# Order of the high and low products in the gate and up projections of a hybrid decoder layer

## The chip, the cores and the metric

The kernel runs on one core of a Trainium2 chip. The metric is the device time of one execution in microseconds (us). Three runs of the kernel before took 1007.79, 1008.01 and 1008.3 us; their median, 1008.01 us, is the time before.

The engines are named as the profile names them: PE is TensorE's matrix products, PEld its weight loads, DVE is VectorE, ACT is ScalarE, POOL is GpSimd, SP is the engine whose queue issues most loads. A "product" is one matmul instruction: 128 x 128 weights, with 256 or 512 columns of activations streamed past them.

## The reference

One decoder layer on 256 tokens of 2048 features, in float32:

```
h = RMSNorm(x);  z = h @ w_in
y = concat(pool mixer, latent attention of 8 heads, attention of 4 heads to 256 memory tokens) @ w_o
x = x + y
h2 = RMSNorm(x)
g = h2 @ w_gate ;  gc = conv_b + sum over j of conv_w[j] * (g shifted by 2 - j tokens)
x = x + (silu(gc) * (h2 @ w_up)) @ w_down
```

`w_gate` and `w_up` are 2048 x 5632, `w_down` is 5632 x 2048. With 44 features tiles of 128 columns, gate and up are 44 x 2 x 16 blocks of 128 x 128 weights.

## The kernel before

**High and low.** Every operand of the large products is split into a high part, rounded to the type fp32r, and a low part, the rest. A product is made of three: high weight by high activation, high weight by low activation, and low weight by high activation. The activations `h2` lie in SBUF as 256 high columns followed by 256 low columns, so that a *high product* (`psm<-h,wh`) streams 512 columns past a block of high weights, and a *low product* (`psm<-h,wl`) streams 256 columns past a block of low weights and adds to the second half of the same PSUM bank. `halves` (L767 on) adds the two halves later.

**From memory to weights.** `load_w` (L82) brings 128 x 2048 floats, 1 MB, into one of three buffers `wr` by SP's queue: a whole features tile of gate or of up. It is split in two pieces of 1024 columns, eight blocks each. For each piece ScalarE writes `wh` by a copy that rounds (L98), and VectorE subtracts it from the raw weights into `wl` (L99). There are three buffers `wh` and three buffers `wl`; a piece occupies one of each until its last product has read it.

**Where the low piece starts.** A buffer `wl` is 64 floats longer than a piece. `gemm_t` (L103) puts the first low piece of a features tile 48 floats (192 bytes) into its buffer and the second one 16 floats (64 bytes). All other weights start at the beginning of their buffers.

**Order.** `gemm_t` runs the first piece high, then low, and the second low, then high. Up follows gate with the same order:

| | piece 0 | piece 1 |
|---|---|---|
| gate | 8 high, 8 low | 8 low, 8 high |
| up | 8 high, 8 low | 8 low, 8 high |

So the loop over f (L817) is a sequence of runs of 16 high and 16 low products. Tile f=0 is done in two parts: the first pieces of gate and up, then the last transposes of the activations, then the second pieces. The input projections (ten features tiles of `w_z`, with the activations `xg`) use `gemm_t` too, and between their two pieces steps of the memory attention are put.

**After a features tile.** `glu` (L774) takes the two PSUM banks: ScalarE copies and VectorE adds the halves (L770, L771), scales, does the three-tap convolution (L778, L780), silu (L781) and the product with up. In 13 of the 22 pairs of features tiles the result is split into `aT` (L144, L145). In the nine pairs of `SEVEN` the second tile of the pair also makes sums and differences of 128 x 128 blocks (`s<-s`, L799) and splits 896 columns at once into `aS` (L802, L803), for a down projection with seven block products where eight would be plain.

**What sets the order of instructions.** Each engine works through its own queue in order. A planner fills the queues ahead of time: it plays the program through with estimated durations, and each engine takes the earliest instruction in the program's order that is ready, including a free buffer for its output. An instruction marked by `keep` stays behind everything written before it on its engine. The gate and up products, splits and `glu` are not marked. PSUM has four banks `psm`, so that gate and up of two features tiles can be under way.

**Other names.** `rxb` (the input's scale for every token, used by the pool mixer) and `krr` (the rotated rope keys) are small tiles of the pool `mix`. `ssacc` is the buffer in which the squares of the memory tokens are summed.

Of the kernel before, what the change touches and what calls it, by code (L numbers as in the profile page):

```python
# [11 lines left out]
F32 = mybir.dt.float32  # L12
F32R = mybir.dt.float32r
BF16 = mybir.dt.bfloat16
AF = mybir.ActivationFunctionType
ALU = mybir.AluOpType
AX = mybir.AxisListType

P = 128
T = 256  # L20
NT = 2
D = 2048
KD = D // P
H = 8
NOPE = 128
ROPE = 64
# [10 lines left out]
STG = 2048  # L37
HS = 1024
# [22 lines left out]
def layer(ctx, tc, xT_d, xn_d, memT_d, vec_d, tab_d, w_z_d, w_mqkr_d, w_q_d, w_kv_d, w_mem_d, w_pool_d, w_o_d,  # L61
          w_g_d, w_u_d, w_dn_d, out_d):
    nc = tc.nc

    const = ctx.enter_context(tc.tile_pool(name="const", bufs=1))
    stage = ctx.enter_context(tc.tile_pool(name="stage", bufs=1))
# [5 lines left out]
    def nm(s):  # L72
        uid[0] += 1
        return f"{s}_{uid[0]}"

    def ps_main():
        return psm.tile([P, 512], F32, tag="m", name=nm("psm"))

    def ps_aux():
        return psa.tile([P, 512], F32, tag="a", name=nm("psa"))  # L80

    def load_w(src, n, cut=STG):  # L82
        raw = stage.tile([P, STG], F32, tag="wr", name=nm("wr"), bufs=3)
        for c in range(0, n, cut):
            nc.sync.dma_start(raw[:, c:min(n, c + cut)], src[:, c:min(n, c + cut)])
        return raw[:]

    def keep(ins, on=True):

        return tc.keep_in_program_order(ins) if on else ins  # L90

    def split_w(raw, o, n, cut=HS, kept=False, shift=0):

        hi = stage.tile([P, HS], F32R, tag="wh", name=nm("wh"), bufs=3)
        lo = stage.tile([P, HS + 64], F32R, tag="wl", name=nm("wl"), bufs=3)[:, shift:shift + HS]
        for c in range(0, n, cut):
            e = min(n, c + cut)
            keep(nc.scalar.copy(hi[:, c:e], raw[:, o + c:o + e]), kept)  # L98
            keep(nc.vector.tensor_tensor(lo[:, c:e], raw[:, o + c:o + e], hi[:, c:e].bitcast(F32), op=ALU.subtract),  # L99
                 kept)  # L100
        return hi, lo

    def gemm_t(ps, raw, o, act, ks, first=True, last=True, kept=False, between=None):  # L103


        ks = list(ks)
        nk = HS // P
        cs = range(0, len(ks), nk)
        for c in cs:
            kc = ks[c:c + nk]  # L110

            hi, lo = split_w(raw, o + c * P, len(kc) * P, shift=16 if c // nk % 2 else 48)

            for low in ((False, True) if c // nk % 2 == 0 else (True, False)):
                for i, k in enumerate(kc):
                    w = (lo if low else hi)[:, i * P:(i + 1) * P]
                    keep(nc.tensor.matmul(ps[:, T if low else 0:2 * T], w, act(k)[:, 0:T] if low else act(k),  # L117
                                          start=first and c + i == 0 and not low,
                                          stop=last and c == cs[-1] and i == len(kc) - 1 and low == (c // nk % 2 == 0),
                                          skip_group_check=True), kept)  # L120
            if between is not None and c == 0:
                between()

    def gemm_n(pss, hi, lo, act, k0, first, last, kept=False, by_span=False):

        nk, n = hi.shape[1], hi.shape[2]
        nj = len(pss[0])
        w = n // nj
        order = [(tt, j) for tt in range(NT) for j in range(nj)]
        if by_span:  # L130
            order.sort(key=lambda x: x[1])
        for i in range(nk):
            for tt, j in order:
                xh = act[:, k0 + i, tt * P:(tt + 1) * P]
                xl = act[:, k0 + i, T + tt * P:T + (tt + 1) * P]
                ps, o = pss[tt][j], slice(j * w, (j + 1) * w)
                keep(nc.tensor.matmul(ps, xh, hi[:, i, o], start=first and i == 0, stop=False), kept)  # L137
                keep(nc.tensor.matmul(ps, xl, hi[:, i, o], start=False, stop=False), kept)  # L138
                keep(nc.tensor.matmul(ps, xh, lo[:, i, o], start=False, stop=last and i == nk - 1), kept)  # L139
# [26 lines left out]
    def rsqrt_(dst, src, scale):  # L166

        nc.scalar.activation(dst, src, AF.Sqrt, bias=eps[:], scale=scale)
        nc.vector.reciprocal(dst, dst)
# [3 lines left out]
    mp = mix.enter_context(tc.tile_pool(name="mix", bufs=1))  # L173
# [7 lines left out]
    def sm(n):  # L181
        o = so[0]
        so[0] += n
        return small[:, o:o + n]

    def tok():
        return mp.tile([P, 512], F32, tag="tok", name=nm("tok"), bufs=3)
# [30 lines left out]
    def head_sq(dst, src):  # L218

        sq = mp.tile([P, 512], F32, tag="hsq", name=nm("hsq"), bufs=2)  # L220
        s3 = sq[:, :src.shape[1] * src.shape[2]].rearrange("p (h d) -> p h d", h=src.shape[1])
        nc.scalar.activation(s3, src, AF.Square)
        nc.vector.tensor_reduce(dst, s3, axis=AX.X, op=ALU.add)
# [31 lines left out]
    ps = ps_aux()  # L255
# [24 lines left out]
    pss = [[ps_main()[:] for _ in range(2)] for _ in range(NT)]  # L280
    for c in range(KD // 2):
        raw = raw0 if c == 0 else load_w(w_mem_d[c], STG, HS if c == 1 else STG)
# [4 lines left out]
        for i in range(2):  # L287
            k = 2 * c + i
            mem_parts(k, k + 1)
            hi, lo = split_w(raw, i * HS, HS, 512 if c == 0 else HS, True)  # L290
# [8 lines left out]
    ps = ps_aux()  # L299
# [41 lines left out]
    def x_load():  # L341
        i = len(x_pieces)
        sq = s4()[:].rearrange("p a t -> p (a t)")
        nc.gpsimd.dma_start(sq, xn_d[i // 2][:, (i % 2) * HS:(i % 2 + 1) * HS])
        x_pieces.append(sq)
# [5 lines left out]
    def x_rstd():  # L351
        keep(nc.vector.tensor_reduce(rx, ssq_x.rearrange("p (t h) -> p t h", h=2), axis=AX.X, op=ALU.add))
        rsqrt_(rx, rx, 1.0 / D)
        nc.vector.tensor_tensor(rx2, rx, rx, op=ALU.mult)
# [6 lines left out]
    pss = [[ps_aux()[:, :NH] for _ in range(2)] for _ in range(NT)]  # L361
    for c in range(KD // 2):
        raw = load_w(w_mqkr_d[c], 2 * 576)
        for i in range(2):
            hi, lo = split_w(raw, i * 576, 576)
# [9 lines left out]
            x_square(i)  # L375
        if c < 4:
            x_load()
    rxb = mp.tile([P, T], F32, name="rxb")

    def mq_done():  # L380

        x_rstd()
        for tt in range(NT):
            t = tok()
            nc.scalar.copy(t[:, 0:NH], pss[tt][0][:, :NH])
            nc.scalar.copy(t[:, NH:512], pss[tt][1][:, :512 - NH])
            nc.scalar.copy(kr[:, tt, :], pss[tt][1][:, 512 - NH:NH])
            head_sq(fmq3[:, tt], t[:].rearrange("p (h d) -> p h d", d=XD))
            nc.vector.tensor_scalar(fmq3[:, tt], fmq3[:, tt], rx2[:, tt:tt + 1], None, op0=ALU.mult)
            to_features(mqT, t, tt, XH, gqk[:, 1:2])  # L390
        rsqrt_(fmq, fmq, 1.0 / XD)
        for tt in range(NT):
            nc.vector.tensor_scalar(fmq3[:, tt], fmq3[:, tt], rx[:, tt:tt + 1], 1.0 / math.sqrt(XD),
                                    op0=ALU.mult, op1=ALU.mult)


        dx = tok()
        for tt in range(NT):
            nc.vector.tensor_scalar(dx[:, tt * P:(tt + 1) * P], identf[:], rx[:, tt:tt + 1], None, op0=ALU.mult)
        ps = ps_aux()  # L400
        nc.tensor.matmul(ps[:, 0:T], ones[:], dx[:, 0:T], start=True, stop=True)
        nc.scalar.copy(rxb[:], ps[:, 0:T])


    class Head:
# [75 lines left out]
    for m in range(6):  # L481
        raw = load_w(w_z_d[m], STG)
        if m in (1, 3):
            keep(nc.sync.dma_start(x1n[:, m // 2, :], xn_d[m // 2]))
        ps = ps_main()
# [3 lines left out]
        a = zs[:, m // 4, :]  # L489
        if m % 4 == 0:  # L490
            nc.scalar.activation(a, z[:], AF.Square)
        else:
            t = mp.tile([P, T], F32, tag="hadd", name=nm("zsq"), bufs=3)
# [21 lines left out]
    zp = mp.tile([P, 4, T], F32, name="zp")  # L515
    def pool_in(g):
        raw = load_w(w_z_d[6 + g], STG)
        ps = ps_main()
        gemm_t(ps, raw, 0, lambda k: xg[:, k, :], range(KD), kept=g == 0, between=lambda: mem_steps(6 + g))
        half_add(zp[:, g, :], ps)  # L520
        nc.vector.tensor_tensor(zp[:, g, :], zp[:, g, :], rxb[:], op=ALU.mult)


    def pool_mix():
# [60 lines left out]


    sskr, fk, fkn, fkr = sm(NT), sm(NT * H), sm(NT * H), sm(NT * H)
    krr = mp.tile([P, NT, 1, ROPE], F32, name="krr")
    for tt in range(NT):
        head_sq(sskr[:, tt:tt + 1], kr[:, tt:tt + 1, :])  # L590
        rotate(krr[:, tt], kr[:, tt:tt + 1, :], 1, tt, 1)
# [119 lines left out]
    for n in range(4):  # L711
        pss = [[ps_main()[:]] for _ in range(NT)]
# [7 lines left out]
    h2 = big.tile([P, KD, 2 * T], F32R, tag="act", name="h2")  # L720
# [17 lines left out]
    for n in range(4):  # L738
        pss = [[ps_main()[:]] for _ in range(NT)]
# [66 lines left out]
    raws = [load_w(w[0], STG) for w in (w_g_d, w_u_d)]  # L806
    pss = [ps_main() for _ in range(2)]
# [7 lines left out]
        gemm_t(ps, raw, HS, lambda k: h2[:, k, :], range(8, KD), first=False)  # L815
    glu(0, *pss)
    for f in range(1, KF):  # L817
        pss = []
        for w in (w_g_d, w_u_d):
            raw = load_w(w[f], STG)  # L820
            pss.append(ps_main())
            gemm_t(pss[-1], raw, 0, lambda k: h2[:, k, :], range(KD))
        glu(f, *pss)


# [85 lines left out]
    for c in range(2):  # L911
# [3 lines left out]
        for j in range(PAIRS):  # L915
            kept = c > 0 or j > SEVEN[0]
# [99 lines left out]
```

## Time and profile before

| | |
|---|---|
| median of three runs | 1008.01 us |
| the profiled execution | 1008.52 us |
| its span, first to last instruction | 1006.7 us |
| TensorE busy (products) | 1001.2 us, 99% |
| TensorE weight loads | 863.2 us, 86% |
| VectorE busy | 751.4 us, 75% |
| ScalarE busy | 577.8 us, 57% |
| memory traffic | 198 GB/s over the span |
| high products of gate and up (L117, `h,wh`) | 1408, mean 391 ns |
| low products of gate and up (L117, `h,wl`) | 1408, mean 278 ns |

How to read it: a product's duration counts from its start to the end of its way through the array, and the next product starts long before that. So the mean durations of 391 and 278 ns are not what a product costs; that is the time from one start to the next. A line such as `L99 DVE TENSOR_TENSOR wl<-wr,wh 128x1024 ... x172 | 210.5, 1224` is a group of instructions: line of the program, engine, operation, output and inputs, shape, count, busy microseconds, mean nanoseconds. A row of the windows is a stretch in microseconds from the span's start, its length, the busy time and count of an engine, the granted TensorE clock, the share of the DMA engines and GB/s. A row of the timeline is a start, a length, an engine, a line and an operation, with the number of instructions merged into it, and in brackets the engine's idle time before it and what ended that.

### The profile page before, as it was taken

How to read it: one execution, taken by the hardware profiler on the slowest of the kernel's cores; microseconds unless marked ns; L12 is line 12 of the kernel's file. 1: busy time of each engine (PE TensorE's matmuls, PEld its weight loads, DVE VectorE, ACT ScalarE, POOL GpSimd, SP SyncE). 2: the span in 40 equal slices, each digit the busy share in tenths (PEclk: the TensorE clock that was granted, in tenths of full speed). 3: DMA queues.
4: the chain of work that ended last, by engine and by line, in shares of the span. 5: the costliest groups of instructions: out<-in, count | busy, mean ns of one | idle time of the engine just before them, and what ended most of it. 6: DMA issues, size and time to landing. Idle time of an engine off the chain costs nothing.

```text
span 1006.7 us, 14129 instructions
## 1 busy us (share of the span) xinstructions
PE 1001.2 (99%) x5354; PEld 863.2 (86%) x5354; DVE 751.4 (75%) x1134; ACT 577.8 (57%) x853; POOL 18.5 (2%) x39
## 2 busy tenths in 40 slices
PE   9999999999999999999999999999999999999998
PEld 8898888888888888888888888888888888888886
DVE  6878689855677676776767677676767788888886
ACT  6778666544576555555555555555555565545553
POOL 1010000000000000000000000000000000010000
PEclk9999999999999999999999999999999999999999
DMA  9777344334665555554555555555555765576551
GB/s 361 260 243 297 129 165 178 128 146 145 210 208 210 179 197 193 184 208 172 205 184 195 194 184 209 174 203 185 191 200 201 263 214 191 205 275 212 206 209 42
DMA packets 31764, 200.17 MB, mean 199 GB/s; under 512 B 3664, under 2 KB 4176, under 8 KB 9808
## 3 DMA queue, kind: packets, MB, share of 16 engines
q1 hardware_dynamic: 28512, 189.04, 52.9%
q0 software_dynamic: 2752, 9.44, 2.6%
q8 instruction: 42, 0.69, 0.3%
q10 hardware_dynamic: 432, 0.79, 0.3%
q14 instruction: 26, 0.21, 0.1%
HBM read 195.06 MB, written 4.19 MB: 198 GB/s over the span
## 4 chain that ended last, share of the span: by engine, by line
PE 99%; DVE 0%; ACT 0%; issue 0%
PE psm L117 53%; PE psm L137 5%; PE psm L138 5%; PE psm L139 5%; PE psa L846 4%; PE psm L844 4%; PE psm L845 4%; PE psa L844 4%; PE psa L845 4%; PE psm L846 4%; PE psa L665 1%; PE psa L137 1%; PE psa L139 1%; PE psa L138 1%; PE psa L229 1%; PE psa L257 1%
## 5 line engine op out<-in xcount | busy, mean ns | idle before, releaser
L99 DVE TENSOR_TENSOR wl<-wr,wh 128x1024 fp32r<-128x1024 f32 (+2 forms) x338 | 392.3, 1165 | 63.7 <-ACT wh L98 58.7
L98 ACT CAST wh<-wr 128x1024 fp32r<-128x1024 f32 (+2 forms) x338 | 339.4, 1006 | 136.2 <-PE psm L138 47.3
L117 PE MATMUL psm<-h,wh 128*128 128x512 f32 x1408 | 336.8, 391 | 0.0
L117 PEld LDWEIGHTS psm<-h,wh 128*128 128x128 f32 x1408 | 257.7, 188 | 50.0
L117 PEld LDWEIGHTS psm<-h,wl 128*128 128x128 f32 x1408 | 176.1, 188 | 6.9
L117 PE MATMUL psm<-h,wl 128*128 128x256 f32 x1408 | 177.5, 278 | 0.0
L99 DVE TENSOR_TENSOR wl<-dn,wh 128x1024 fp32r<-128x1024 f32 x58 | 67.8, 1220 | 26.3 <-ACT wh L98 26.3
L98 ACT CAST wh<-dn 128x1024 fp32r<-128x1024 f32 x58 | 59.3, 1052 | 38.3 <-PE psm L845 21.7
L770 ACT COPY g<-psm 128x256 f32<-128x256 f32 x44 | 16.4, 372 | 88.7 <-PE psm L117 88.7
L771 DVE TENSOR_TENSOR g<-g,psm 128x256 f32<-128x256 f32 x44 | 18.5, 420 | 58.7 <-ACT g L770 58.7
L771 DVE TENSOR_TENSOR u<-u,psm 128x256 f32<-128x256 f32 x44 | 18.5, 421 | 52.8 <-ACT u L770 52.8
L781 ACT ACTIVATE gc<-gc 128x256 f32<-128x256 f32 x44 | 18.4, 419 | 63.9 <-DVE gc L780 63.8
L780 DVE SCALAR_TENSOR_TENSOR gc<-g,vec,gc 128x255 f32<-128x255 f32 x88 | 42.1, 478 | 0.3
L844 PE MATMUL psa<-wh,aT 128*128 128x512 f32 x104 | 40.5, 389 | 0.0
L845 PE MATMUL psa<-wh,aT 128*128 128x512 f32 x104 | 40.5, 389 | 0.0
L845 PE MATMUL psm<-wh,aT 128*128 128x512 f32 x104 | 40.5, 389 | 0.0
L846 PE MATMUL psa<-wl,aT 128*128 128x512 f32 x104 | 40.5, 389 | 0.0
L844 PE MATMUL psm<-wh,aT 128*128 128x512 f32 x104 | 40.5, 389 | 0.0
L846 PE MATMUL psm<-wl,aT 128*128 128x512 f32 x104 | 40.5, 389 | 0.0
L117 PE MATMUL psm<-xg,wh 128*128 128x512 f32 x160 | 39.9, 393 | 0.0
L137 PE MATMUL psm<-wh,cat 128*128 128x512 f32 x96 | 38.2, 398 | 0.0
L139 PE MATMUL psm<-wl,cat 128*128 128x512 f32 x96 | 37.4, 390 | 0.0
(227 smaller groups left out, 1393.9 us busy)
## 6 DMA issues: line engine op xcount, KB each, us to landing
wr<-in_w_g SPq DMA_DIRECT2D x44, 1024.0 KB, 4.8
wr<-in_w_u SPq DMA_DIRECT2D x44, 1024.0 KB, 4.8
wr<-in_w_dn SPq DMA_DIRECT2D x33, 1024.0 KB, 4.8
wr<-in_w_o SPq DMA_DIRECT2D x16, 1024.0 KB, 4.9
dn<-in_w_dn SPq DMA_DIRECT2D x11, 1024.0 KB, 4.9
wr<-in_w_z SPq DMA_DIRECT2D x10, 1024.0 KB, 5.5
wr<-in_w_mem SPq DMA_DIRECT2D x6, 1024.0 KB, 7.8
wr<-in_w_mqkr SPq DMA_DIRECT2D x8, 576.0 KB, 4.0
```

The costliest lines, as they stand in the source:

```text
L98: keep(nc.scalar.copy(hi[:, c:e], raw[:, o + c:o + e]), kept)
L99: keep(nc.vector.tensor_tensor(lo[:, c:e], raw[:, o + c:o + e], hi[:, c:e].bitcast(F32), op=ALU.subtract), kept)
L117: keep(nc.tensor.matmul(ps[:, T if low else 0:2 * T], w, act(k)[:, 0:T] if low else act(k), start=first and c + i == 0 and not low, stop=l ...
L137: keep(nc.tensor.matmul(ps, xh, hi[:, i, o], start=first and i == 0, stop=False), kept)
L138: keep(nc.tensor.matmul(ps, xl, hi[:, i, o], start=False, stop=False), kept)
L139: keep(nc.tensor.matmul(ps, xh, lo[:, i, o], start=False, stop=last and i == nk - 1), kept)
L771: nc.vector.tensor_tensor(t[:], t[:], ps[:, T:2 * T], op=ALU.add)
L780: nc.vector.scalar_tensor_tensor(gc[:, d:T], g[:, 0:T - d], v(w, f), gc[:, d:T], op0=ALU.mult, op1=ALU.add)
L781: nc.scalar.activation(gc[:], gc[:], AF.Silu)
L844: nc.tensor.matmul(ps, a[0], b[0], start=first, stop=False)
L845: nc.tensor.matmul(ps, a[1], b[0], start=False, stop=False)
L846: nc.tensor.matmul(ps, a[0], b[1], start=False, stop=last)
```

## The change

For the tiles f = 1 to 43 a new function `gemm_pair` does gate and up together. Each is split whole, and then gate runs 16 high and 16 low products and up 16 low and 16 high:

| | |
|---|---|
| gate | 16 high, 16 low |
| up | 16 low, 16 high |

A new function `split_t` replaces `split_w` in `gemm_t` and serves `gemm_pair`. It writes a low piece in two halves of four blocks, by one subtraction whose output has a gap, and each half has its own offset in the buffer, given modulo 64 floats. The first low piece of gate (and the first of each `gemm_t`) has its first half at 192 bytes and its second half at 64 bytes more than a multiple of 256; all other low pieces have both halves at 64. The buffers `wl` grow by 64 floats to 1152. To make room, `rxb` and `krr` move into one tile `late` that takes the buffer of `ssacc`.

```diff
-    def split_w(raw, o, n, cut=HS, kept=False, shift=0):
+    def split_w(raw, o, n, cut=HS, kept=False):
...
-        lo = stage.tile([P, HS + 64], F32R, tag="wl", name=nm("wl"), bufs=3)[:, shift:shift + HS]
+        lo = stage.tile([P, HS + 128], F32R, tag="wl", name=nm("wl"), bufs=3)[:, 0:HS]
...
+    def split_t(raw, o, n, low, kept):
+        hi = stage.tile([P, HS], F32R, tag="wh", name=nm("wh"), bufs=3)
+        lo = stage.tile([P, HS + 128], F32R, tag="wl", name=nm("wl"), bufs=3)
+        d = n // 2 + (low[1] - low[0] - n // 2) % 64
+        lo2 = lo[:, low[0]:low[0] + 2 * d].rearrange("p (a n) -> p a n", a=2)[:, :, 0:n // 2]
+        half = lambda t: t.rearrange("p (a n) -> p a n", a=2)
+        keep(nc.scalar.copy(hi[:, :n], raw[:, o:o + n]), kept)
+        keep(nc.vector.tensor_tensor(lo2, half(raw[:, o:o + n]), half(hi[:, :n]).bitcast(F32), op=ALU.subtract), kept)
+        m = n // P
+        return ([hi[:, i * P:(i + 1) * P] for i in range(m)],
+                [lo2[:, i // (m // 2), i % (m // 2) * P:(i % (m // 2) + 1) * P] for i in range(m)])
...
     def gemm_t(ps, raw, o, act, ks, first=True, last=True, kept=False, between=None):
...
-            hi, lo = split_w(raw, o + c * P, len(kc) * P, shift=16 if c // nk % 2 else 48)
+            hi, lo = split_t(raw, o + c * P, len(kc) * P, (16, 16) if c // nk % 2 else (48, 16), kept)
...
-                    w = (lo if low else hi)[:, i * P:(i + 1) * P]
+                    w = (lo if low else hi)[i]
...
+    def gemm_pair(pss, raws, act):
+        nk = HS // P
+        for s, (ps, raw) in enumerate(zip(pss, raws)):
+            parts = [split_t(raw, c * HS, HS, (48, 16) if s + c == 0 else (16, 16), False) for c in range(KD // nk)]
+            for low in ((False, True) if s == 0 else (True, False)):
+                for k in range(KD):
+                    nc.tensor.matmul(ps[:, T if low else 0:2 * T], parts[k // nk][low][k % nk],
+                                     act(k)[:, 0:T] if low else act(k), start=k == 0 and low == (s == 1),
+                                     stop=k == KD - 1 and low == (s == 0), skip_group_check=True)
...
-    rxb = mp.tile([P, T], F32, name="rxb")
+    late = mp.tile([P, 2, T], F32, tag="ssacc", name="late", bufs=1)
+    rxb = late[:, 0, :]
...
-    krr = mp.tile([P, NT, 1, ROPE], F32, name="krr")
+    krr = late[:, 1, 0:NT * ROPE].rearrange("p (t o d) -> p t o d", t=NT, o=1)
...
     for f in range(1, KF):
-        pss = []
-        for w in (w_g_d, w_u_d):
-            raw = load_w(w[f], STG)
-            pss.append(ps_main())
-            gemm_t(pss[-1], raw, 0, lambda k: h2[:, k, :], range(KD))
+        pss = [ps_main() for _ in range(2)]
+        gemm_pair(pss, [load_w(w[f], STG) for w in (w_g_d, w_u_d)], lambda k: h2[:, k, :])
         glu(f, *pss)
```

More of the change, by code (lines that the diff above doesn't have):

```diff
@@ L401, in mq_done @@
         nc.tensor.matmul(ps[:, 0:T], ones[:], dx[:, 0:T], start=True, stop=True)
-        nc.scalar.copy(rxb[:], ps[:, 0:T])
+        nc.scalar.copy(rxb, ps[:, 0:T])
     class Head:
@@ L520, in pool_in @@
         half_add(zp[:, g, :], ps)
-        nc.vector.tensor_tensor(zp[:, g, :], zp[:, g, :], rxb[:], op=ALU.mult)
+        nc.vector.tensor_tensor(zp[:, g, :], zp[:, g, :], rxb, op=ALU.mult)
     def pool_mix():
```

## The prediction

> **What bounds the kernel now.** I read the profile page first, for the busy shares, the chain that ended last and the clock.
>
> ```profile
> span 1006.7 us, 14129 instructions
> ...
> PE 1001.2 (99%) x5354; PEld 863.2 (86%) x5354; DVE 751.4 (75%) x1134; ACT 577.8 (57%) x853; POOL 18.5 (2%) x39
> ...
> PEclk9999999999999999999999999999999999999999
> ...
> PE 99%; DVE 0%; ACT 0%; issue 0%
> ```
>
> TensorE never rests and its clock never falls below nine tenths (the windows below have 1.00), so only the time from one product to the next counts. A busy share of 99% does not say that this time is at its least. So I next listed the groups in the stretch from the first product of tile f=1 to the first of the down projection, and then read the order of the products, and two blocks of other work, in the timeline.
>
> ```profile
> L117 PE MATMUL psm<-h,wh 128*128 128x512 f32 x1376 | 328.3, 391 | 0.0
> L99 DVE TENSOR_TENSOR wl<-wr,wh 128x1024 fp32r<-128x1024 f32 x172 | 210.5, 1224 | 6.4 <-ACT wh L98 1.9
> L98 ACT CAST wh<-wr 128x1024 fp32r<-128x1024 f32 x172 | 180.9, 1052 | 12.3 <-PE psm L117 10.2
> L117 PE MATMUL psm<-h,wl 128*128 128x256 f32 x1378 | 173.4, 278 | 0.0
> ```
>
> ```profile
> 501.54 2.01 PE L117 MATMUL psm<-h,wl 128*128 128x256 f32 x16
> 503.38 3.81 PE L117 MATMUL psm<-h,wh 128*128 128x512 f32 x16
> 507.04 2.01 PE L117 MATMUL psm<-h,wl 128*128 128x256 f32 x16
> 508.88 3.81 PE L117 MATMUL psm<-h,wh 128*128 128x512 f32 x16
> ```
>
> Gate and up of one features tile are 32 high and 32 low products, in runs of 16, with four changes of kind. I then set windows on single weight tiles, with bounds at the starts of products; each has 8 products unless I say otherwise (the count in brackets also takes in neighbours that run over a bound).
>
> ```profile
> 501.54:502.48 0.94, 0.94 (x9) 1.00 1.03 436
> 502.48:503.38 0.91, 0.91 (x10) 1.00 0.98 415
> 503.38:505.22 1.84, 1.84 (x10) 1.00 0.30 58
> 505.22:507.04 1.81, 1.81 (x9) 1.00 0.79 298
> 127.02:132.46 5.44, 5.44 (x25) 1.00 0.30 123
> 94.83:95.66 0.82, 0.82 (x9) 1.00 0.00 0
> 88.87:89.11 0.24, 0.24 (x4) 1.00 0.50 207
> 89.11:89.68 0.57, 0.57 (x7) 1.00 0.11 43
> 304.46:305.38 0.93, 0.93 (x10) 1.00 1.00 416
> 301.66:774.73 473.07, 473.07 (x2755) 1.00 0.54 192
> ```
>
> In order: a low tile at 192 bytes takes 0.94 us (117.5 ns each); the next, at 64 bytes, 0.91; the first high tile after lows 1.84; the second 1.81. Two such sets make 11.00, and the last row gives 473.07 / 43 = 11.00 us per features tile: the four numbers are the whole tile. The 24 products of the fifth row go at 226.7 ns; half of that, 113.3, is the pace of 0.91. So a tile is 32 x (0.2267 + 0.1133) = 10.88 us of plain pace and **0.12 us of losses: 0.03 twice for a low tile at 192 bytes and 0.03 twice for the first highs after lows.** The DMA share moves from 1.03 to 0.30 beside them without a trace in the pace.
>
> The next three rows are why the low tiles have two offsets. Seven products at 64 bytes that follow a break of other work (sixth row) stay at 0.82 / 7 = 117 ns. In another such tile two take 0.24 us, and the next five 0.57, which is 114 each. So 64 bytes is not quick by itself: it has a slow and a quick state. Behind a tile at 192 bytes every one in the long loop is quick.
>
> **The change, part by part.** *Order.* Gate high, high, low, low, and up low, low, high, high leave one low run of 32 and one high run of 32: two changes of kind instead of four. One loss of 0.03 after lows goes. Products, their number and their shapes stay.
>
> *Offsets.* A run starts with half a tile at 192 bytes, 4 products for 8, and goes on at 64. Of the two losses of 0.03 at 192 bytes, one goes whole and half of the other. Losses per tile are then 0.015 + 0.03, and 0.075 us go. 43 x 0.075 = **-3.2 us**. What no row shows is whether four products bring on the quick state as eight do. From below it costs nothing and the four are quick too: 43 x 0.015 = 0.65 more gain. From above, the run of 304.46 (eight products at 64 bytes that begin in another state) takes 0.93, 0.02 over the quick 0.91: 43 x 0.02 = 0.9 less. Beyond that is a rival. I take zero, for the 86 regular turns from 192 to 64 bytes are nearest. In the ten tiles of the input projection and the four first halves of f=0, half of a first low tile becomes quick: 14 x 0.015 = **-0.2 us**.
>
> *The split into two halves* is one subtraction whose output has a gap. Not shown; whole it takes 1224 ns, and two of half the length (first row below, from the groups; the others are of two tiles' instructions) would take 1370. I take 1224, the same elements in one instruction; either hides.
>
> ```profile
> L99 DVE TENSOR_TENSOR wl<-wr,wh 128x512 fp32r<-128x512 f32 x22 | 15.0, 685 | 0.6 <-ACT wh L98 0.5
> ...
> L402 ACT COPY rxb<-psa x1: 359/359/359, 82.9 to 82.9; 128x256 f32<-128x256 f32 x1
> ...
> L216 PE MATMUL psa<-ones,ssacc x4: 164/250/250, 50.3 to 50.5; 128*128 128x1 f32 x4
> ```
>
> *rxb and krr* move into the buffer of ssacc, whose last reader is at 50.5, while rxb is first written at 82.9: a wait met 32 us earlier, nothing. The stage pool grows by 768 bytes and shifts later buffers by multiples of 256. The low buffers already start 4352 bytes apart, so they alternate by 256 within 512 bytes without a mark in the loop: nothing.
>
> *Buffers.* Here is a new cost. Four low tiles now run back to back on three low buffers: the fourth (up's second) can be subtracted only when gate's first is read. A low product lasts 278 ns where the next starts after 113, so the buffer is free 0.17 us after the next tile starts.
>
> ```profile
> 500.86 0.84 PE L117 MATMUL psm<-h,wh 128*128 128x512 f32 x3
> ...
> 501.74 1.05 ACT L98 CAST wh<-wr 128x1024 fp32r<-128x1024 f32 x1
> ```
>
> ```profile
> 532.92 0.37 ACT L770 COPY u<-psm 128x256 f32<-128x256 f32 x1 [0.42 <-PE psm L117]
> 533.19 1.06 ACT L98 CAST wh<-wr 128x1024 fp32r<-128x1024 f32 x1
> 533.33 0.42 DVE L771 TENSOR_TENSOR u<-u,psm 128x256 f32<-128x256 f32 x1 [1.33 <-ACT u L770]
> ...
> 534.24 0.29 DVE L799 TENSOR_TENSOR s<-s 128x128 f32<-128x128 f32 x1
> ...
> 534.45 1.22 DVE L99 TENSOR_TENSOR wl<-wr,wh 128x1024 fp32r<-128x1024 f32 x1
> ...
> 535.59 0.28 DVE L799 TENSOR_TENSOR s<-s 128x128 f32<-128x128 f32 x1
> ...
> 536.27 3.27 PEld L117 LDWEIGHTS psm<-h,wh 128*128 128x128 f32 x15
> 536.38 3.36 PE L117 MATMUL psm<-h,wh 128*128 128x512 f32 x14
> ...
> 537.28 0.94 ACT L802 CAST aS<-s 128x896 fp32r<-128x896 f32 x1 [1.49 <-DVE s L799]
> 538.26 1.09 DVE L803 TENSOR_TENSOR aS<-s,aS 128x896 fp32r<-128x896 f32 x1 [1.01 <-ACT aS L802]
> ```
>
> These are rows of the timeline. The cast of 501.74 starts 0.04 us after its buffer's reader ended (500.86 + 0.84). So release and start take 0.21, the subtraction 1.22, about 0.04 more reaches TensorE, and a weight load starts 0.11 ahead of its product (536.27 against 536.38): 1.58 us, against 1.82 for the two low tiles between. **It fits with 0.24 us to spare**, if VectorE is free then. Behind the waiting subtraction stand glu's steps and the next tile's subtractions; no product needs those before the next low run, 8 us on.
>
> VectorE is not free in the nine tiles that follow an odd tile of a seven-product pair. There the tile starts at 532.72 (the u copy less 0.2) and the first low buffer would come free 3.63 + 0.93 + 0.2 later, at 537.48. The s steps no longer wait behind a second subtraction: 535.59, the last by 536.2, the aS cast until 537.2, the aS subtraction from 537.2 to 538.3. It starts 0.3 before the buffer is free, and the low tile is late by 0.8 - 0.24 = 0.56 us. The planner of the order knows of such waits and puts other ready products there, as it did here at the start of f=1:
>
> ```profile
> 299.77 1.10 PE L117 MATMUL psm<-h,wh 128*128 128x512 f32 x4
> ...
> 300.72 1.10 PE L117 MATMUL psm<-h,wl 128*128 128x256 f32 x8
> ```
>
> So I expect no stall but two or three highs of the next gate inside the low run: 0.02 for the highs and 0.03 for eight slow lows, 9 x 0.05 = **+0.45 us**. Loads: up's raw buffer comes free with that subtraction, at 6 us into a tile, and its next use is the cast for the gate two tiles on, 8.7 us later; a megabyte lands in 4.8 us (a row of the DMA issues): nothing.
>
> ```profile
> wr<-in_w_g SPq DMA_DIRECT2D x44, 1024.0 KB, 4.8
> ```
>
> Sum: -3.2 - 0.2 + 0.45 = **-3.0 us**. The profiled execution took 1008.52 with its span of 1006.7, 1.8 lying around it; it should come to 1005.5 with a span of 1003.7. The median of the runs, 1008.01, is 0.5 below the profiled one: **1005.0 us**.
>
> **The rivals.** *Slow by count.* The eight slow lows might belong to the change of kind and not to the offset. For it: they are always the first eight. Against it: 89.11, quick after three. Then half the tile at 64 bytes saves nothing, and a tile gains 0.06: -2.6 + 0.45, **1005.9**. The Trainium skill would point here: "TensorE: Matmul & The Clock Gate", step-by-step part on loading weights, says that the array has two independent read ports and that loading the next weights takes nothing from the running product. By that rule an offset of weights could not matter at all. The row 94.83 against 502.48, the same shape and offset at 117 and 113 ns, sits ill with it, but does not exclude it.
>
> *Not caught.* Four products do not bring on the quick state and the whole run stays at 117.5 (94.83 for it, 304.46 against): 32 x 0.1175 = 3.76 us for now 2 x 1.85 = 3.70. +0.06 - 0.03 for the one change saved is +0.03 a tile: 43 x 0.03 = +1.3, and 0.3 for the nine: **1009.6**.
>
> *Slower: the fourth low tile is late.* Nothing bridges the wait in the nine tiles: 9 x 0.56 = 5.0 where aS starts 0.3 ahead, up to 9 x (1.09 - 0.24) = 7.6 where it starts just ahead. Net of 3.4, **1009.6 to 1012.2**, 1010.9 in the middle. It decides once VectorE is taken for over 0.24 us when gate's first low buffer comes free. For it: VectorE is 75% busy; against it: 299.77.
>
> *The order is not what the text says.* If the planner finds the fourth tile late in every features tile, it breaks every run, two changes come back, and with them 0.06 or more of 0.075: **1007.5**.
>
> **How the numbers follow.** Forecast 58%, its own range 1004.0 to 1006.0 from the bounds above; by count 10%; not caught 10%; late 13%; order broken 9%. A measurement tells 0.2%, 2 us, from no change. Faster by more: 55 of the forecast and 7 of the count, 62%. Slower by more: 9 of late, 4 of not caught, 2 of the broken order, 15%. Within: 23%. The range runs from 1003.9 to 1009.8, where it leaves out the upper half of late and some tails.
>
> **What would show it.** Runs of 32 in the timeline; about 10.93 us from one features tile to the next; after the first four lows 113 ns, the fifth to eighth above all; 0.03 after lows once a tile; idle TensorE before a low tile, or highs between lows, only in tiles after seven-product pairs. A low run of 3.76 throws out the forecast, and so does TensorE waiting for VectorE's wl.

## The result

The changed kernel takes 1075.68 us (median of five runs, 1074.64 to 1076.3), the kernel before 1008.01. The ratio is 1.0668, 95% interval 1.0653 to 1.0684: 67.7 us **slower**, where 3.0 us faster was forecast. These are rows of the changed kernel's page.

```profile
span 1072.9 us, 14013 instructions
...
PE 1027.2 (96%) x5354; PEld 879.5 (82%) x5354; DVE 751.9 (70%) x1134; ACT 580.6 (54%) x853; POOL 18.5 (2%) x39
...
PE   9995666999999999999999999999999999999998
...
PEclk9998778999999999999999999999999999999999
...
PE 94%; ACT 3%; DVE 1%; DMA 1%; issue 0%; ACTq 0%
```

The same 5354 products, but TensorE is now idle for 45.7 us of the span (5.5 before), most of it between 75 and 200 us, and its granted clock falls there. That is the input projection, which the prediction had passed over with a gain of 0.2 us. Windows from the projection's first product to its last, and from the first product of f=1 to the first of the down projection, give the account (columns: stretch, length, then busy time and count of PE, PEld, DVE, ACT and POOL, or of PE alone; granted clock, DMA share, GB/s). First the kernel before:

```profile
77.38:163.90 86.52, 86.46 (x491) 74.72 (x490) 68.91 (x154) 60.52 (x114) 0.00 (x0) 1.00 0.52 190
```

Then the changed kernel:

```profile
76.78:225.72 148.94, 108.70 (x491) 89.53 (x490) 71.17 (x154) 61.66 (x114) 0.00 (x0) 0.84 0.30 109
363.46:840.84 477.37, 477.37 (x2754) 1.00 0.53 190
```

The projection grew by 148.94 - 86.52 = 62.4 us, the loop over features tiles by 477.37 - 473.07 = 4.3. Together 66.7, against 66.2 between the two spans; the projection starts 0.6 us earlier than before (76.78 against 77.38). Of the 62.4, 40.2 is idle TensorE (148.94 - 108.70), and 22.2 is longer busy time.

Who was waited for in the changed kernel's projection (total us, times, longest):

```profile
PE psm L132 <- DVE wl L112: 23.2, 6, 5.1
PE psm L132 <- ACT wh L111: 13.7, 5, 2.8
PE psm L165 <- ACT wh L98: 3.4, 1, 3.4
```

The three rows make up the 40.2 us; the third is one product of the next matrix, which the planner had put between those of the projection. The kernel before has no row for PE in that view. The timeline shows what stood ahead of the splits. First ScalarE in the kernel before:

```profile
86.65 1.03 ACT L98 CAST wh<-wr 128x1024 fp32r<-128x1024 f32 x1
87.70 1.28 ACT L423 ACT_TABLE_LOAD   x1
90.04 0.56 ACT L423 ACTIVATE p<-psa,st,small 128x256 f32<-128x256 f32 x1 [1.05 <-DVE st L421]
```

The changed kernel, all engines:

```profile
96.59 0.57 ACT L453 ACTIVATE p<-psa,st,small 128x256 f32<-128x256 f32 x1 [5.61 <-DVE st L451]
...
98.23 0.56 ACT L453 ACTIVATE p<-psa,st,small 128x256 f32<-128x256 f32 x1
...
98.77 1.04 ACT L111 CAST wh<-wr 128x1024 fp32r<-128x1024 f32 x1
...
99.85 1.22 DVE L112 TENSOR_TENSOR wl<-wr,wh 128x1024 fp32r<-128x1024 f32 x1
...
101.13 1.22 PE L132 MATMUL psm<-xg,wl 128*128 128x256 f32 x4 [5.10 <-DVE wl L112]
```

Before, a cast for the next products ran ahead of the attention step's exponentials. Now the cast stands behind all of them, ScalarE sits idle 5.61 us at their head, and the subtraction and the products follow one after the other. The diff says why in one word: `split_w` was called in `gemm_t` without `kept` and so was free in the order; `split_t` is called with it, and `kept` is true for seven of the ten projection tiles. This is in the diff as printed above, and the prediction did not see it.

### The profile page after: what moved, and what is told of

Its sections match the earlier page's. It is cut to its first block, busy times and chain, and to the rows that moved or that the text cites. A ratio compares the mean times of both kernels' runs of the same rounds, so it can differ in the third digit from the quotient of the medians.

```text
span 1072.9 us, 14013 instructions
## 1 busy us (share of the span) xinstructions
PE 1027.2 (96%) x5354; PEld 879.5 (82%) x5354; DVE 751.9 (70%) x1134; ACT 580.6 (54%) x853; POOL 18.5 (2%) x39
## 4 chain that ended last, share of the span: by engine, by line
PE 94%; ACT 3%; DVE 1%; DMA 1%; issue 0%; ACTq 0%
PE psm L148 44%; PE psm L132 8%; PE psm L165 5%; PE psm L167 5%; PE psm L166 5%; PE psm L873 4%; PE psa L873 4%; PE psm L872 4%; PE psa L872 4%; PE psa L871 4%; PE psm L871 4%; ACT wh L111 1%; PE psa L695 1%; DVE wl L112 1%; DMA wr<-in_w_z 1%; PE psa L471 1%
## 5 line engine op out<-in xcount | busy, mean ns | idle before, releaser
L148 PE MATMUL psm<-h,wh 128*128 128x512 f32 x1376 | 321.6, 390 | 0.0
L112 DVE TENSOR_TENSOR wl<-wr,wh 128x1024 fp32r<-128x1024 f32 x196 | 236.8, 1223 | 107.4 <-PE psm L148 55.9
L111 ACT CAST wh<-wr 128x1024 fp32r<-128x1024 f32 x196 | 205.6, 1050 | 75.8 <-PE psm L148 59.4
L98 ACT CAST wh<-wr 128x1024 fp32r<-128x1024 f32 (+2 forms) x142 | 133.4, 942 | 114.3 <-PE psm L166 40.0
L99 DVE TENSOR_TENSOR wl<-wr,wh 128x1024 fp32r<-128x1024 f32 (+2 forms) x142 | 152.7, 1085 | 46.9 <-ACT wh L98 46.6
L808 ACT ACTIVATE gc<-g,vec 128x256 f32<-128x256 f32 x44 | 26.5, 601 | 92.2 <-DVE g L806 92.2
L132 PE MATMUL psm<-xg,wh 128*128 128x512 f32 x160 | 54.1, 491 | 13.7 <-ACT wh L111 13.7
L132 PEld LDWEIGHTS psm<-xg,wh 128*128 128x128 f32 x160 | 37.5, 246 | 24.2 <-ACT wh L111 16.4
L132 PE MATMUL psm<-xg,wl 128*128 128x256 f32 x160 | 28.3, 334 | 23.2 <-DVE wl L112 23.2
L132 PEld LDWEIGHTS psm<-xg,wl 128*128 128x128 f32 x160 | 26.8, 239 | 26.2 <-DVE wl L112 25.0
```

The costliest lines, as they stand in the source:

```text
L111: keep(nc.scalar.copy(hi[:, :n], raw[:, o:o + n]), kept)
L112: keep(nc.vector.tensor_tensor(lo2, half(raw[:, o:o + n]), half(hi[:, :n]).bitcast(F32), op=ALU.subtract), kept)
L148: nc.tensor.matmul(ps[:, T if low else 0:2 * T], parts[k // nk][low][k % nk], act(k)[:, 0:T] if low else act(k), start=k == 0 and low == ( ...
```

## The experiments

**The kept splits.** The edit takes one argument back:

```diff
-            hi, lo = split_t(raw, o + c * P, len(kc) * P, (16, 16) if c // nk % 2 else (48, 16), kept)
+            hi, lo = split_t(raw, o + c * P, len(kc) * P, (16, 16) if c // nk % 2 else (48, 16), False)
```

> The changed kernel, but the copies and subtractions of the input projection are free in the order again, as they were before the change (the products stay kept in order). Theory: holding these splits in program order is what lengthened the input projection from 86.5 to 148.9 us; then this run has the projection at 86.5 again, and only the loop's loss of 4.3 us is left: 1012.1 to 1012.4 us. Rival: the tile that rxb and krr now share, or the subtraction in two halves, is what the projection waits for; then it stays near 149 us and the time near 1075.

1012.71 us (four executions), ratio 1.0043 (1.0026 to 1.006). The other way round, the kernel before with that argument alone:

```diff
-            hi, lo = split_w(raw, o + c * P, len(kc) * P, shift=16 if c // nk % 2 else 48)
+            hi, lo = split_w(raw, o + c * P, len(kc) * P, kept=kept, shift=16 if c // nk % 2 else 48)
```

> The kernel before, with one thing of the change: the copies and subtractions of the input projection are kept in program order. Theory of the kept splits: the projection takes about 149 us, and the time is 1008 + 62 = 1070 us. Rival (shared tile or halves): 1008 us, since neither is in it.

1072.95 us (two executions, 1070.51 and 1075.39), ratio 1.0641 (1.0613 to 1.0669). The projection's window of the first run:

```profile
77.08:163.75 86.67, 86.67 (x491) 74.94 (x490) 69.14 (x154) 60.64 (x114) 0.00 (x0) 1.00 0.53 191
```

and of the second:

```profile
76.74:225.91 149.17, 108.91 (x491) 89.59 (x490) 71.20 (x154) 61.63 (x114) 0.00 (x0) 0.84 0.30 110
```

So the kept splits account for the whole of the 62 us, and neither the shared tile `late` nor the two halves take part. What is left, 1012.71 against the 1008.03 that the kernel before took beside it, is the loop, which takes 477.49 us here and 473.07 before:

```profile
301.51:779.00 477.49, 477.29 (x2754) 1.00 0.53 190
```

**Which number of products at 192 bytes.** First the changed kernel's own loop, one tile with a whole run of 32 lows: four products at 192 bytes, 28 at 64, then the first eight highs.

```profile
589.16:589.63 0.47, 0.47 (x5) 1.00 0.78 330
589.63:592.92 3.30, 3.30 (x30) 1.00 0.37 124
592.92:594.76 1.84, 1.84 (x10) 1.00 0.83 312
```

3.30 / 28 = 117.8 ns: the quick state never comes. This window and those below are of one features tile each; in each of these runs at least 33 of the 43 tiles have the same length within 0.01 us. All further runs have the free splits. With the whole first piece at 192 bytes,

```diff
-            parts = [split_t(raw, c * HS, HS, (48, 16) if s + c == 0 else (16, 16), False) for c in range(KD // nk)]
+            parts = [split_t(raw, c * HS, HS, (48, 48) if s + c == 0 else (16, 16), False) for c in range(KD // nk)]
```

> The kernel of the first run of this call with the whole first low piece of a run at 192 bytes, eight products, and the other 24 at 64. Theory: four products do not bring on the quick state, eight do; a low run is 0.94 + 24 x 0.1134 = 3.66 us, a features tile 10.94 instead of 11.05 us, and the time is 1012.3 - 43 x 0.105 = 1007.8 us (the nine tiles with a high product inside the low run keep their 0.25 us each). Rival: it is the order, with 32 lows in one run over two PSUM banks, that does not come into the quick state; then the tile stays at 11.05 us and the time at 1012.3.

```profile
525.33:526.27 0.94, 0.94 (x9) 1.00 1.02 418
526.27:528.99 2.72, 2.72 (x26) 1.00 0.28 84
```

2.72 / 24 = 113.3 ns, 10.94 us a tile, as expected; the time is 1009.09 us, ratio 1.001 (1.0001 to 1.002), 1.3 more than expected, mostly because the nine tiles with a broken run cost more now (below). The same question in the order of before, where the loop over f has the old `gemm_t` calls with the halves at 192 and 64:

```diff
-        pss = [ps_main() for _ in range(2)]
-        gemm_pair(pss, [load_w(w[f], STG) for w in (w_g_d, w_u_d)], lambda k: h2[:, k, :])
+        pss = []
+        for w in (w_g_d, w_u_d):
+            raw = load_w(w[f], STG)
+            pss.append(ps_main())
+            gemm_t(pss[-1], raw, 0, lambda k: h2[:, k, :], range(KD))
```

> The order of before (8 high, 8 low, 8 low, 8 high for each of gate and up), with the first low piece in two halves at 192 and 64 bytes as in the change, and the splits free. Theory that four products at 192 bytes are too few: all 16 lows stay at 117.5 ns, a features tile takes 11.00 + 2 x 0.034 = 11.07 us, and the time is about 1010.9 us. Rival that the order is at fault: the run is quick from the fifth low on, 11.00 - 2 x 0.015 = 10.97 us a tile and 1006.7 us.

```profile
525.08:526.49 1.42, 1.42 (x14) 1.00 0.45 185
```

These are the twelve lows behind the first four: 118 ns each, 11.08 us a tile, and 1011.44 us, ratio 1.0032 (1.002 to 1.0044). Four are too few in either order, so the order is not at fault.

Why four and not eight? In the traces the slow lows repeat in threes (117.5, 117.5, 118.3 ns from start to start, as means over the whole runs), so the place in that step at which the offset changes might decide. To choose a number n freely, the first low piece of a run is written by two subtractions:

```diff
+        nc.vector.tensor_tensor(lo[:, 48:48 + c], raw[:, o:o + c], hi[:, 0:c].bitcast(F32), op=ALU.subtract)
+        nc.vector.tensor_tensor(lo[:, 80 + c:80 + HS], raw[:, o + c:o + HS], hi[:, c:HS].bitcast(F32), op=ALU.subtract)
```

with `c` = n x 128. Five:

> As the run with eight products at 192 bytes, but five products at 192 bytes and the other 27 of the run at 64; the first low piece is written by two subtractions for this (five blocks and three). Theory of the step of three: slow low products come in threes (117.5, 117.5, 118.3 ns), and the change of offset is caught where it falls at one place of the three. Eight is caught, four is not; five has the remainder of eight by three, so it is caught: 113 ns from the sixth or seventh low on, about 10.93 us a features tile. Rivals: a least number of products between five and eight is needed, or the change must fall on the border of two pieces; then the whole run stays at 117.5 and the tile at 11.05 us.

```profile
525.49:526.07 0.59, 0.59 (x6) 1.00 1.05 447
526.07:529.13 3.06, 3.06 (x29) 1.00 0.48 120
```

Two:

> The same with two products at 192 bytes and 30 at 64. Theory of the step of three: two has the remainder of eight by three and is caught, 10.92 us a features tile. Rivals of a least number or of the border: 11.05 us.

```profile
524.99:528.39 3.40, 3.40 (x32) 1.00 0.50 154
```

None at 192 (all 32 at 64 bytes, in one subtraction a piece):

> All 32 low products of a run at 64 bytes, nothing at 192. If the offset of 192 bytes is what brings on the quick state behind it, the run stays at 117.5 ns and the tile at 11.05 us (as in the changed kernel: its half tile at 192 is then without effect). If 192 bytes is merely slow and has no part in it, the run is quick throughout and the tile at 10.91 us.

```profile
527.43:531.20 3.77, 3.77 (x33) 1.00 0.44 152
```

These three kernels, and the next two, were executed once each, so that the windows and not the times decide. Five gives 3.06 / 27 = 113.3 ns behind them, 10.93 us a tile and 1008.82 us; two gives 3.40 / 30 = 113.3, 10.91 and 1007.83; none gives 3.77 / 32 = 117.8, 11.05 and 1013.1. Rivals of a least number or of the border between pieces are out: two is fewer than four and lies within a piece. Then two that the step of three should not catch. Three:

> Three products at 192 bytes, 29 at 64, in the new order. Theory of the step of three (the change of offset is caught after 2, 5 and 8 products, remainder two by three): three has remainder nought and is not caught; the run stays at 117.5 ns and the tile at 11.05 us. Rival: every number but four is caught, four being an accident of the half tile; then 10.92 us.

```profile
525.70:529.00 3.30, 3.30 (x31) 1.00 0.31 117
526.06:529.00 2.95, 2.95 (x28) 1.00 0.25 89
```

Seven:

> Seven products at 192 bytes, 25 at 64. Step of three: seven has the remainder of four, not caught, 11.05 us a tile. Rival of every number but four: 10.94 us.

```profile
527.39:530.33 2.94, 2.94 (x27) 1.00 0.26 78
```

Seven is not caught: 2.94 / 25 = 117.6 ns, 11.05 us a tile, 1011.89 us. Three missed the expectation: the first three behind the change take 0.357 us in the trace, 119 ns each, and the 26 after them 2.95 / 26 = 113.5; the tile is 10.93 us, and the time 1008.78. So what the runs show is narrower than the theory: two, five and eight are caught at once, three only behind three more slow products, four and seven not. Both numbers that fail leave one by three; one and six were not run. That a remainder of nought fails too was wrong.

**The nine tiles.** In the changed kernel every tile that follows an odd tile of a seven-product pair has the run 24 low, 1 high, 8 low. Its timeline there (tile start 507.71):

```profile
511.27 0.95 ACT L832 CAST aS<-s 128x896 fp32r<-128x896 f32 x1 [0.49 <-DVE s L829]
511.34 2.99 PE L148 MATMUL psm<-h,wl 128*128 128x256 f32 x24
...
512.25 1.09 DVE L833 TENSOR_TENSOR aS<-s,aS 128x896 fp32r<-128x896 f32 x1 [1.01 <-ACT aS L832]
513.26 1.22 DVE L112 TENSOR_TENSOR wl<-wr,wh 128x1024 fp32r<-128x1024 f32 x1
...
514.16 0.39 PE L148 MATMUL psm<-h,wh 128*128 128x512 f32 x1
...
514.53 1.00 PEld L148 LDWEIGHTS psm<-h,wl 128*128 128x128 f32 x8 [0.29 <-DVE wl L112]
```

The first low buffer comes free at 511.34 + 0.94 + 0.2 = 512.48, and aS took VectorE at 512.25. The tile's fourth subtraction starts 0.8 us late, the planner puts one high product in, and TensorE's weight load still waits 0.29. In the next run aS is written behind the next tile's splits and its subtraction is kept there (on the kernel with eight at 192 bytes):

```diff
-            nc.scalar.copy(hi, sf)
-            nc.vector.tensor_tensor(lo, sf, hi.bitcast(F32), op=ALU.subtract)
+            def rest():
+                nc.scalar.copy(hi, sf)
+                keep(nc.vector.tensor_tensor(lo, sf, hi.bitcast(F32), op=ALU.subtract))
+            later.append(rest)
...
         gemm_pair(pss, [load_w(w[f], STG) for w in (w_g_d, w_u_d)], lambda k: h2[:, k, :])
+        while later:
+            later.pop()()
```

> The kernel with eight products at 192 bytes, and in the nine odd tiles of seven-product pairs the split of 896 columns into aS is written behind the next tile's splits and its subtraction kept there on VectorE. Theory: that subtraction taking VectorE just before the first low buffer is free is what puts a high product into the low run and costs 0.25 to 0.35 us in each of the nine tiles; then all runs are of 32, every features tile takes 10.94 us, the loop 43 x 10.94 + 0.3 = 470.7 us against 473.07 before, and the time is 1005.7 us. Rival: the fourth low tile is late for another cause (the buffer alone); then the nine tiles still take 11.2 us or more, and the time stays at 1008 to 1009.

```profile
301.39:772.08 470.69, 470.69 (x2754) 1.00 0.54 193
```

All runs are of 32, 42 of the 43 tiles take 10.94 us and the first 11.21, and the time is 1005.57 us, ratio 0.9976 (0.9967 to 0.9985).

**Everything together, and the offset alone.** With two products at 192 bytes and aS kept behind:

> The new order, free splits, two products at 192 bytes, and the split into aS kept behind the next tile's splits: everything that was found. All runs of 32, 10.91 us a features tile, the loop 43 x 10.913 + 0.3 = 469.6 us against 473.07, and the time 1004.4 us, 3.6 us under the kernel before. If the two subtractions of the first low piece or the wait for the low buffer disturb the order, single tiles stand out at 11.2 us or more and the time is nearer 1006.

```profile
301.20:770.99 469.78, 469.78 (x2754) 1.00 0.54 193
```

1004.77 us, ratio 0.9967 (0.9954 to 0.9979), 3.4 us under the 1008.16 that the kernel before took beside it. And the order of before, with two products at 192 bytes instead of eight and the splits free (the first low pieces of the projection have two as well, since `gemm_t` makes them):

> The order of before with two products at 192 bytes in each run of 16 lows instead of eight. If the offset alone carries part of what the change was after, a features tile takes 11.00 - 2 x 6 x 0.0043 = 10.95 us and the time is 1008.0 - 2.2 = 1005.8 us; the new order is then worth 0.03 to 0.04 us a tile by itself. If the catch after two depends on the new order, the tile goes to 11.08 us and the time to 1011.4.

```profile
522.23:523.82 1.59, 1.59 (x16) 1.00 0.66 273
301.23:771.96 470.73, 470.73 (x2754) 1.00 0.55 193
```

1.59 / 14 = 113.6 ns behind the first two, 10.95 us a tile, 1005.48 us, ratio 0.9974 (0.9964 to 0.9984). Some seven tenths of the loop's gain, 2.3 of 3.3 us, come from the offset in the old order; the new order and the move of aS together add 0.95 us (470.73 - 469.78). The new order without that move does not pay. This is the loop of the run above with two products at 192 bytes and aS where the change leaves it:

```profile
301.06:774.01 472.94, 472.24 (x2754) 1.00 0.54 192
```

It takes 2.2 us more than the old order with the same offsets (472.94 against 470.73), because of the nine tiles. In the old order no tile stands out (42 of the 43 take 10.95 us), so little is left there for the move of aS to save; it was not run.

A version with a fourth low buffer, which would test the buffer by itself, was not run.

## Why the prediction was wrong, point by point

**The step that failed first** is "In the ten tiles of the input projection and the four first halves of f=0, half of a first low tile becomes quick: 14 x 0.015 = -0.2 us". It costed the offsets there and not the call. The call hands `kept` on to two instructions that were free before, and the runs put 62 us on that: nine tenths of the miss. No rival covered it, since all of them were about the loop.

**"What no row shows is whether four products bring on the quick state as eight do ... I take zero, for the 86 regular turns from 192 to 64 bytes are nearest."** Wrong, and the reason given was weak: all 86 turns come after eight products, so they are one case and not 86. The rival "Not caught" is what happened. Its size was off too: +0.03 us a tile from windows rounded to 0.01, where the tile went from 11.00 to 11.05, and 0.3 us for the nine tiles, which took 2.2.

**"One loss of 0.03 after lows goes."** Right: highs after lows still take 1.84, once a tile. Between the run with two in the new order and that in the old one, 10.95 - 10.91 = 0.04 us a tile, of which about 0.01 is the second pair of products at 192 bytes.

**"It fits with 0.24 us to spare."** Right for 33 of the 43 tiles, which take 11.05 us without a wait. **The nine tiles**: the place and the cause were right (aS ahead of the buffer by 0.3 forecast, 0.23 measured; late by 0.8, as forecast), and the planner did put a high product there. The price, 0.05 us a tile, was too low: 11.29 against 11.05 is 0.24, for the one high did not fill the wait. With the quick state it is 0.35 to 0.38 (11.29 against 10.94 with eight products at 192 bytes, against 10.91 with two), probably because the run then asks for its fourth tile earlier. The changed kernel's 4.3 us in the loop are 2.0 of the slow state (43 x 0.047, one change of kind less included), 2.2 of the nine tiles and 0.1 of the first tile.

**"Slow by count"** falls: none at 192 bytes leaves all 32 slow, two make 30 quick. With it falls, for this kernel, what was concluded there from the rule of the Trainium skill ("TensorE: Matmul & The Clock Gate", the step on loading weights), that an offset of weights could not matter: the runs with four and with eight products at 192 bytes have the same products in the same order, and behind the eight a product takes 4.5 ns less through the addresses of the weights alone (113.3 against 117.8). Whether the two read ports disturb each other, which is what the rule itself denies, no run shows. **"Late"** did not happen as a stall of 0.56 us; the wait that was left is 0.29 us. **"Order broken"** happened in nine tiles, not in all.

**The forecast's sum for the loop, "-3.2 ... + 0.45",** does not stand even where the quick state comes, and the term that fails there is the 0.45. With two products at 192 bytes a whole tile takes 10.91 us, 0.09 under 11.00 where 0.075 was taken off. But the nine tiles cost 9 x 0.38 = 3.4 us and the first one 0.2, and the loop comes to 472.94 against 473.07. So with the free splits and the quick state that the prediction counted on, the change would by that run have been worth next to nothing; the 469.78 needs the move of aS, which the change does not make.

## What to carry to other kernels

Read every argument of a changed call, not only the one that the change is about: one that pins two small instructions to the program's order can cost twenty times what the change was after (62 us against 3). Where a long row of equal events supports a claim, ask in how many different ways it came about; here 86 were one. When three buffers serve four tiles in a row, find which instruction takes the filling engine just before the first buffer comes free, and put it behind.

## What was not expected of the hardware

**The pace of products has two states**, and which one holds depends on how many products ran at another weight offset before: after 0, 4 or 7 of them at 192 bytes the lows at 64 bytes take 117.6 to 118 ns, after 2, 3, 5 or 8 they take 113.3 to 113.6, and each state lasts for the rest of the run. The weight loads show it too: with none at 192 bytes, 405 of the loop's 1376 loads of low weights take 192 ns where the others take 186 to 189, and with two at 192 bytes only 4 do. What in the memory or the array does this was not tried.

**The clock followed the idle time.** The projection's granted clock was 0.84 in the changed kernel. In one stretch behind a wait of 2.70 us (a row of the timeline) it was 0.52, then 1.00 again (windows):

```profile
89.73 3.62 PE L132 MATMUL psm<-xg,wh 128*128 128x512 f32 x8 [2.70 <-ACT wh L111]
```

```profile
89.73:93.19 3.46, 3.46 (x8) 0.52 0.26 106
93.31:94.13 0.83, 0.83 (x9) 1.00 0.00 0
```

The first row's eight high products take 3.46 / 8 = 433 ns each, against 226.7 at the full clock. The Trainium skill ("TensorE: Matmul & The Clock Gate", the part on the clock gate) says that an idle window of some 3.4 us halves the clock until TensorE has been busy for about as long. These rows agree with the half clock and with how long it lasted, for it was over within the 3.46 us. They do not agree with the length of the idle window: a wait of 2.70 us was enough here.

The clock explains that busy time grew too. A granted clock of 0.84 over the projection stands for 148.94 x 0.16 = 24 us lost, an estimate from that row; part of it fell into the waits, and 22.2 of the 62 us are longer busy time.
